# Two unused tiles that put the operands of every large matmul at multiples of 512 bytes

## The chip, the cores and the metric

The kernel runs on one core of one Trainium2 chip. The metric is device time in microseconds (us) of one execution; before the change the median of three runs is 2399.38 us (2398.85 to 2400.38).

## The reference

One decoder layer on 2048 tokens of width 1024, in float32. What matters here is that it is a chain of large matrix products, all of which TensorE computes:

```
h = rms_norm(x, norm_w) * (1 + scale) + shift          # shift, scale, gate = silu(c) @ w_ada + b_ada
z = h @ w_in                                            # 1024 -> 10240 columns
a, b, g_conv, q, k, v, g_attn, m_conv, m_attn = split(z)
u = silu(layer_norm(causal_conv31(a * sigmoid(b)))) * silu(g_conv)
y_conv = u @ w_conv_out
o = merge(dilated_attention(rope(norm(q)), rope(norm(k)), v))   # 12 heads, 3 dilations
y_attn = (o * silu(g_attn)) @ w_attn_out
y = sigmoid(m_conv) * y_conv + sigmoid(m_attn) * y_attn
out = x + gate * (y @ w_out)
```

## The kernel before

Every large product is made in three terms: each operand is split into a high part of type fp32r and the fp32r remainder (tiles with hi/lo or h/l in their names), and high*high, high*low and low*high are summed in one PSUM bank. One matmul loads a stationary operand of 128x128 and streams a moving operand past it, 384 or 512 columns wide. The order of TensorE's instructions is written out by hand (`tc.manual_schedule`), so PE goes through the program as it stands; the other engines are ordered by the tile scheduler. The stages, in order of time:

1. **Start** (L120 to L225): the condition vector, the angles of the rotary table, the first tokens' norms. Tiles in the pools `start` and `xp`.
2. **Token projection with attention** (L371, 4608 matmuls of 384 columns): 12 heads by 16 blocks of 128 tokens, 24 matmuls each into `pz`. Stationary is a 128-token slice of `hT_hi`/`hT_lo` (pools `hT0`, `hT1`), moving the weights `wh_u`/`wl_u` (pools `wp0`, `wp1`). Between the matmuls of a block stand those of attention: `ptq` (L436), `ps` (L451), `ptp` (L468) and `po` (L500), plain float32 of 128 columns, on tiles of the pool `wk` and the constant `ident`.
3. **Quads** (L897, 3696 matmuls of 512 columns): the convolution's and the gates' columns, two column blocks by two token blocks in seven products instead of eight (tiles A, S for tokens, B, T for weights), 12 matmuls a product. Moving are the token quarters in `hT0`/`hT1`, stationary the weights `sh`/`sl` in the pool `ws`.
4. **Projections back** (L1203, 1152 matmuls of 512 columns): 32 blocks `ya` of 12 matmuls, then 32 blocks `yc` of 24. Moving are the attention's or the convolution's output (`ai`, `u` in the pools `ub` and `ua`; for the first 8 `ya` blocks `ai0` in `hT0`), stationary `wa` and `wc` (in `hT0` and `wcp`). Beside them VectorE and ScalarE normalise the convolution's output for the next token quarter, which PE needs in two small steps, `pc` (L1239) and `pr` (L1248), and prepare the last stage's weights (`wo_raw`, L1349 and L1354).
5. **Output** (L1485, 672 matmuls of 512 columns): 8 quads of seven products of 12 matmuls into `oa`, `ob`, `oc`. Stationary is `y` (pool `ub`, the first two products `op`), moving the seven weight tiles `wo`: B11 in `lnp`, T2, B22 and T4 in `hT0`, T3 in `wcp`, B21 and T1 in `op`.

SBUF is given out as two stacks: pools opened without a side grow up from the low addresses ("left"), those with `side="right"` grow down from the top ("right"). A tile's start address is therefore the sum of what lies beneath it on its own side. The lines that set this around the change:

```
tab = tabs.tile([P, NB, 2, 64], F32, tag="tab", name="tab0")          # L120
with pool("start", side="right") as st:                               # L121
...
hpool_c = [tc.tile_pool(name=f"hT{i}", bufs=1, side="right", reuse_waits="tile") for i in range(2)]
...
gpa_c.__exit__(None, None, None)                                      # L1170
cv_c.__exit__(None, None, None)
gp = ctx.enter_context(pool("gt", bufs=3))
big["fr"] = ctx.enter_context(pool("fr", bufs=2))
...
wcp_c, wcp = right("wcp")
lnp_c, lnp = right("lnp")
ys_c = pool("ys", bufs=2)
up_c = [pool("ub"), pool("ua")]
...
            nc.tensor.matmul(pz, w, xx, start=(m == 0), stop=(m == len(terms) - 1))   # L1203
```

The three 512-column stages differ in nothing but tiles: L897, L1203 and L1485 all are a loop over 12 or 24 terms, with the next stationary operand loaded while the present moving one streams.

Of the kernel before, what the change touches and what calls it, by code (L numbers as in the profile page):

```python
# [10 lines left out]
F32 = mybir.dt.float32  # L11
# [7 lines left out]
P = 128  # L19
# [35 lines left out]
def tile_hybrid_block(  # L55
# [9 lines left out]
    def pool(name, bufs=1, **kw):  # L65
        return tc.tile_pool(name=name, bufs=bufs, reuse_waits="tile", **kw)
# [51 lines left out]
    tabs = tabs_c.__enter__()  # L118

    tab = tabs.tile([P, NB, 2, 64], F32, tag="tab", name="tab0")  # L120
    with pool("start", side="right") as st:  # L121
        keep = tc.keep_in_program_order
        nat = st.tile([4 * KC, P], F32, name="nat")
# [467 lines left out]
    side = {}  # L591
# [577 lines left out]
    assert not conv_todo  # L1169
    gpa_c.__exit__(None, None, None)  # L1170
    cv_c.__exit__(None, None, None)
    gp = ctx.enter_context(pool("gt", bufs=3))
    big["fr"] = ctx.enter_context(pool("fr", bufs=2))
    pe_order.__exit__(None, None, None)
# [399 lines left out]
```

## Time and profile before

| | |
|---|---|
| median of three runs | 2399.38 us |
| the profiled execution's own time | 2401.62 us |
| its span, first to last instruction | 2399.8 us |
| mean granted TensorE clock | 0.993 |
| PE / weight loads / VectorE / ScalarE / GpSimd busy | 98% / 87% / 72% / 43% / 35% |

Busy times of PE cannot be added to a time, since matmuls are pipelined and overlap: one of 512 columns is shown for some 0.39 us while the next starts 0.23 us after it. What a matmul costs is read from start to start, or from the chain of waits: there each piece is a run of the same kind, with its length and its count, and length divided by count is the price of one.

### The profile page before, as it was taken

What the parts mean: (1) busy time and instruction counts of PE and PEld (TensorE: products, weight loads), DVE (VectorE), ACT (ScalarE), POOL (GpSimd) and SP (SyncE); (2) the same over time, 40 slices, a digit from 0 to 9 for tenths busy, and PEclk for the clock granted to TensorE, in tenths of its full rate; (3) what the DMA queues carried; (4) which work ended last, traced back from release to release, by engine and by line L of the source; (5) the groups of instructions that cost most, each with busy time, mean ns of one, the idle gap of its engine ahead of it and who ended that gap; (6) DMA issues with size and microseconds to landing.
All of it is one profiled execution on the core that took longest, in us unless ns stands there. A gap on an engine that the chain in (4) does not pass through costs nothing.

```text
span 2399.8 us, 38725 instructions
## 1 busy us (share of the span) xinstructions
PE 2356.1 (98%) x12353; PEld 2089.2 (87%) x12353; DVE 1738.8 (72%) x4091; ACT 1022.4 (43%) x2850; POOL 842.7 (35%) x1003
## 2 busy tenths in 40 slices
PE   6999999999999999999999999999999999999999
PEld 2989999999999999998888888788888888878887
DVE  5865655655556777777699999979968778787544
ACT  4733433333444454456444444644444444332221
POOL 3421111111111111123667779656556730000221
PEclk8999999999999999999999999999999999999999
DMA  7633544555552222134545455745444579866552
GB/s 258 216 118 105 163 124 143 155 151 155 165 161 79 65 79 62 55 108 156 169 133 176 154 158 193 239 127 152 141 149 132 167 228 319 288 230 200 177 158 101
DMA packets 354105, 378.56 MB, mean 158 GB/s; under 512 B 29736, under 2 KB 251208, under 8 KB 353902
## 3 DMA queue, kind: packets, MB, share of 16 engines
q1 hardware_dynamic: 316414, 316.64, 42.4%
q10 hardware_dynamic: 37488, 59.46, 7.3%
q8 instruction: 98, 1.61, 0.3%
q14 instruction: 105, 0.86, 0.1%
HBM read 235.34 MB, written 140.64 MB: 157 GB/s over the span
## 4 chain that ended last, share of the span: by engine, by line
PE 87%; DVE 3%; DMA 2%; ACT 2%; issue 1%; POOL 1%; SPq 0%; ACTq 0%; DVEq 0%; POOLq 0%
PE pz L371 29%; PE paab L897 7%; PE yc L1203 6%; PE oa L1485 4%; PE ya L1203 4%; PE pcab L897 4%; PE pag_mc_d L897 4%; PE pag_g_d L897 3%; PE pag_ma_d L897 3%; PE po L500 3%; PE ps L451 3%; PE oc L1485 2%; PE pcg_g_d L897 2%; PE pcg_mc_d L897 2%; PE paag L897 2%; PE pbab L897 2%
## 5 line engine op out<-in xcount | busy, mean ns | idle before, releaser
L371 PE MATMUL pz<-wh_u,hT_lo 128*128 128x384 f32 x1536 | 536.8, 350 | 5.4 <-DVE hT_lo L290 3.6
L371 PE MATMUL pz<-wh_u,hT_hi 128*128 128x384 f32 x1536 | 518.7, 338 | 4.8 <-ACT wh_u L347 2.4
L371 PE MATMUL pz<-wl_u,hT_hi 128*128 128x384 f32 x1536 | 519.2, 338 | 0.4 <-DVE wl_u L350 0.4
L114 POOL TENSOR_SCALAR st<-st 128x2 f32<-128x2 f32 x192 | 48.6, 253 | 809.8 <-ACT sq L388 809.8
L402 DVE SCALAR_TENSOR_TENSOR qk<-pz,st,wqk 128x128 f32<-128x128 f32 x384 | 116.9, 346 | 270.7 <-POOL st L115 269.6
L371 PEld LDWEIGHTS pz<-wh_u,hT_hi 128*128 128x128 f32 x1536 | 291.0, 189 | 8.0 <-ACT wh_u L347 3.3
L371 PEld LDWEIGHTS pz<-wh_u,hT_lo 128*128 128x128 f32 x1536 | 290.0, 189 | 8.3 <-DVE hT_lo L290 4.6
L371 PEld LDWEIGHTS pz<-wl_u,hT_hi 128*128 128x128 f32 x1536 | 290.0, 189 | 1.6 <-DVE wl_u L350 1.1
L443 ACT ACTIVATE qkT<-ptq 128x256 f32<-128x256 f32 x192 | 73.5, 383 | 358.3 <-PE ptq L436 304.0
L975 DVE SCALAR_TENSOR_TENSOR ce<-us,pair_taps,ce 128x512 f32<-128x512 f32 x240 | 180.6, 753 | 6.5
L946 DVE SCALAR_TENSOR_TENSOR ce<-ut,chan,ce 128x512 f32<-128x512 f32 x240 | 178.7, 745 | 0.0
L861 POOL TENSOR_TENSOR slT<-wT,shT 128x512 fp32r<-128x512 f32 x107 | 143.7, 1344 | 81.0 <-ACT shT L860 81.0
L959 DVE SCALAR_TENSOR_TENSOR cq<-ut,chan,cq 128x512 f32<-128x512 f32 x208 | 155.2, 746 | 1.0
L860 ACT ACTIVATE shB<-wB 128x512 fp32r<-128x512 f32 x130 | 82.0, 631 | 162.7 <-PE paab L897 51.7
L115 POOL TENSOR_TENSOR st<-st,mhalf 128x2 f32<-128x2 f32 x192 | 137.3, 715 | 16.0
L388 ACT ACTIVATE sq<-pz 128x128 bf16<-128x128 f32 x384 | 105.6, 275 | 87.5 <-PE pz L371 78.5
L860 ACT ACTIVATE shT<-wT 128x512 fp32r<-128x512 f32 x110 | 69.4, 631 | 163.9 <-POOL wT L852 33.3
L861 POOL TENSOR_TENSOR slB<-wB,shB 128x512 fp32r<-128x512 f32 x85 | 111.0, 1306 | 77.9 <-ACT shB L860 77.4
L500 PE MATMUL po<-lv,pT 128*128 128x128 f32 x596 | 96.8, 274 | 0.0
L500 PEld LDWEIGHTS po<-lv,pT 128*128 128x128 f32 x596 | 90.9, 190 | 0.6 <-issue 0.5
L409 DVE TENSOR_TENSOR t<-qk,tab 128x256 f32<-128x256 f32 x192 | 82.4, 429 | 5.5
L861 POOL TENSOR_TENSOR slT<-wB,shT 128x512 fp32r<-128x512 f32 x57 | 75.1, 1322 | 27.5 <-ACT shT L860 27.4
(742 smaller groups left out, 6162.2 us busy)
## 6 DMA issues: line engine op xcount, KB each, us to landing
wB<-in_w_in_dram SPq DMA_DIRECT2D x154, 256.0 KB, 3.4
qkv_d<-qkv SPq DMA_DIRECT2D x128, 192.0 KB, 2.3
wT<-tT_d SPq DMA_DIRECT2D x88, 256.0 KB, 2.7
raw_u<-in_w_in_dram SPq DMA_DIRECT2D x93, 192.0 KB, 3.4
tT_d<-wB ACTq DMA_DIRECT2D x66, 256.0 KB, 2.3
lqk<-qkv_d SPq DMA_DIRECT2D x128, 128.0 KB, 2.2
acc_d<-osb SPq DMA_DIRECT2D x128, 65.0 KB, 2.0
part<-acc_d ACTq DMA_DIRECT2D x64, 130.0 KB, 2.2
```

Of the source, the lines that this page charges most:

```text
L115: nc.gpsimd.tensor_tensor(dst, scratch[:, :n], mhalf[:, :n], op=ALU.pow)
L371: nc.tensor.matmul(pz[:, :width], part(a, k, P * j, P), w[:, :width], start=(m == 0), stop=(m == 23))
L402: nc.vector.scalar_tensor_tensor(qk[:, 2 * i : 2 * i + 2].rearrange("p a b -> p (a b)"), pz[:, P * i : P * i + P], st[:, 2 + i : 3 + i], w ...
L500: nc.tensor.matmul(po[:, :P], box["pT"][:, P * i : P * i + P], vt, start=(i == 0), stop=(i == nk - 1))
L860: nc.scalar.activation(h, q[name], AF.Copy)
L861: eng.tensor_tensor(l, q[name], h.bitcast(F32), op=ALU.subtract)
L897: nc.tensor.matmul(ps, w, x, start=(m == 0 and ps.name not in first), stop=(m == 11 and not more), skip_group_check=True)
L946: stt(box["e"], e[:, 1 + j : 513 + j], chan[:, cb, 2 * j : 2 * j + 1], box["e"], op0=ALU.mult, op1=ALU.add)
L959: stt(box["o"], o[:, 2 + j : 514 + j], w, psum_o, op0=ALU.mult, op1=ALU.add)
L975: stt(dst, box["both"][:, 1 + j : 513 + j], pair_taps[:, cb, j : j + 1], box["e"], op0=ALU.mult, op1=ALU.subtract if j == 0 else ALU.add)
L1203: nc.tensor.matmul(pz, w, xx, start=(m == 0), stop=(m == len(terms) - 1))
L1485: nc.tensor.matmul(ps, y, w, start=(m == 0 and ps.name not in begun), stop=(m == 11 and not more), skip_group_check=True)
```

## The change

```
@@ -118,6 +118,8 @@
     tabs = tabs_c.__enter__()
 
     tab = tabs.tile([P, NB, 2, 64], F32, tag="tab", name="tab0")
+    edge = ctx.enter_context(pool("edge", side="right"))
+    edge.tile([P, 120], F32, name="edge")
     with pool("start", side="right") as st:
         keep = tc.keep_in_program_order
         nat = st.tile([4 * KC, P], F32, name="nat")
@@ -1169,6 +1171,8 @@
     assert not conv_todo
     gpa_c.__exit__(None, None, None)
     cv_c.__exit__(None, None, None)
+    level = ctx.enter_context(pool("level"))
+    level.tile([P, 32], F32, name="level")
     gp = ctx.enter_context(pool("gt", bufs=3))
     big["fr"] = ctx.enter_context(pool("fr", bufs=2))
     pe_order.__exit__(None, None, None)
```

`edge` takes 480 bytes of each partition at the top and so moves every right-hand tile of the whole program down by 480. `level` takes 128 bytes and moves the left-hand tiles that are opened after the quads (`gt`, `fr`, `ys`, `ub`, `ua`, `ap`, `op`) up by 128. Neither is read or written. On each of the five engines the same instructions on the same tiles stand in the same order before and after; only addresses differ, and a handful of semaphore waits that follow from which older tile a new one overlaps. The start of each operand within 512 bytes, from the two built programs:

| stage | matmuls | moving, before -> after | stationary, before -> after |
|---|---|---|---|
| token projection L371 | 4608 | `wh_u`, `wl_u` 480 -> 0 | `hT` 480 -> 0 |
| quads L897 | 3696 | quarters 480 -> 0 | `sh`, `sl` 480 -> 0 |
| L1203, first 8 `ya` blocks | 96 | `ai0` 480 -> 0 | `wa` 480 -> 0 |
| L1203, the rest | 1056 | `ai`, `u` 384 -> 0 | `wa`, `wc` 480 -> 0 |
| L1485, B11, T2, T3, B22, T4 | 480 | `wo` 480 -> 0 | `y` 384 -> 0 |
| L1485, B21 and T1 | 192 | `wo` 384 -> 0 | `y` 384 -> 0 |
| attention L436 to L500 | | `ident` 128, `wk` tiles 256 and 416, unchanged | the same |

Of the waits, three matter: one fetch `part<-acc_d` (L516, ScalarE's queue, second block of the ninth head) now also waits for the store `s_d` of the last quarter sum; the first `d<-pm,d` (L1229, VectorE) also waits for a GpSimd instruction of the last quad (L923); and the load `yq` (L1395, SyncE's queue) and one `ai` remainder no longer wait for GpSimd.

More of the change, by code (lines that the diff above doesn't have):

```diff
@@ L120, in tile_hybrid_block @@
     tab = tabs.tile([P, NB, 2, 64], F32, tag="tab", name="tab0")
+    edge = ctx.enter_context(pool("edge", side="right"))
+    edge.tile([P, 120], F32, name="edge")
     with pool("start", side="right") as st:
@@ L1171, in tile_hybrid_block @@
     cv_c.__exit__(None, None, None)
+    level = ctx.enter_context(pool("level"))
+    level.tile([P, 32], F32, name="level")
     gp = ctx.enter_context(pool("gt", bufs=3))
```

## The prediction

> **What bounds the kernel.** I read the page first: the busy shares, the clock, and the chain that ended last.
>
> ```profile
> span 2399.8 us, 38725 instructions
> PE 2356.1 (98%) x12353; PEld 2089.2 (87%) x12353; DVE 1738.8 (72%) x4091; ACT 1022.4 (43%) x2850; POOL 842.7 (35%) x1003
> PEclk8999999999999999999999999999999999999999
> ...
> PE 87%; DVE 3%; DMA 2%; ACT 2%; issue 1%; POOL 1%; SPq 0%; ACTq 0%; DVEq 0%; POOLq 0%
> ```
>
> TensorE is the bound: 87% of the chain is PE, at full clock almost everywhere. Nothing in this change adds or removes a matmul, so the only question is whether the price of one matmul depends on where its operands start. For that I read the chain of waits stretch by stretch (columns: start in us, length in us, engine, tile, line, count) and divide length by count. First the quads, where by the table of the change both operands start at 480:
>
> ```profile
> 1302.33 2.72 PE pag_mc_d L897 x12
> ...
> 1326.81 2.72 PE paab L897 x12
> ```
>
> 2.72 us over 12 is 226.7 ns for 512 columns. Now the stage behind it, whose first pieces are of the same shape:
>
> ```profile
> 1960.32 7.26 PE ya L1203 x32
> ...
> 2004.43 33.73 PE ya L1203 x144
> ...
> 2056.27 33.73 PE yc L1203 x144
> ...
> 2146.89 92.78 PE yc L1203 x396
> ```
>
> The first 32 matmuls have `ai0` at 480 against `wa` at 480: 7.26/32 = 226.9 ns, as in the quads. The later ones have the moving operand at 384 against a stationary one at 480: 33.73/144 = 234.2 ns, twice, and 92.78/396 = 234.3 ns. Same stage, same width, same weights `wa`; what differs is where the moving tile lies. Last, the output stage:
>
> ```profile
> 2245.21 2.81 PE oa L1485 x12
> 2248.02 2.76 PE ob L1485 x12
> 2250.78 2.81 PE oa L1485 x12
> ...
> 2262.00 2.76 PE oc L1485 x12
> 2264.76 2.81 PE oa L1485 x12
> ...
> 2396.06 0.69 DVE xt L1472
> ```
>
> Here the stationary `y` is at 384. Products with weights at 480 (all `oa`) take 2.81/12 = 234.2 ns; those with weights at 384 (`ob`, and the `oc` at 2262.00) 2.76/12 = 230.0 ns. Inside such an `ob` the timeline (start, shown length, matmul) tells why it lies between:
>
> ```profile
> 2247.86 0.40 PE L1485 MATMUL ob<-wohB,yh 128*128 128x512 f32 x1
> ...
> 2249.72 0.39 PE L1485 MATMUL ob<-wohB,yl 128*128 128x512 f32 x1
> ...
> 2250.62 0.40 PE L1485 MATMUL oa<-wohT,yh 128*128 128x512 f32 x1
> ```
>
> The first eight steps take 1.86 us, 232.5 ns each; the last four 0.90 us, 225 ns each to the rounding. Equal starts do not give the low price at once: the stream falls into it after some eight matmuls. So I read a rhythm between the two streams, cheap when moving and stationary operand start at the same place within 512 bytes, and reached only after several matmuls. Distance is not the cause: by their addresses the operands of the quads lie 20 to 184 KB apart, those of the dear pairs 59 to 190.
>
> **The change part by part.** `level` and `edge` together bring the 384s and 480s to one value, 0.
>
> *L1203.* 1152 matmuls less the 96 already equal are 1056, at 234.2 - 226.9 = 7.3 ns: **-7.7 us**.
>
> *L1485.* A quad of 84 matmuls recurs every 2264.76 - 2245.21 = 19.55 us. At 2.72 us for 12, it takes 7 x 2.72 = 19.04. That is 0.51 us for each of 8 quads: **-4.1 us**.
>
> Does the whole gain show? Waits of PE in this part, and the stretches where other engines might become late:
>
> ```profile
> PEld pr L1248 <- POOL stf L115: 2.0, 1, 2.0
> ```
>
> ```profile
> 1981.00:2052.00 71.00, 71.00 (x320) 57.50 (x319) 52.60 (x86) 27.31 (x45) 2.90 (x4) 1.00 0.96 326
> 2104.00:2134.00 30.00, 30.00 (x128) 23.80 (x127) 26.70 (x43) 12.57 (x20) 0.00 (x0) 1.00 0.58 193
> 2236.00:2396.00 160.00, 160.00 (x688) 128.89 (x686) 82.59 (x119) 34.06 (x61) 39.52 (x29) 1.00 0.46 147
> ```
>
> ```profile
> 2135.53 9.13 DMA wo_raw<-in_w_out_dram
> 2144.65 1.03 POOL stf L115
> 2145.69 0.04 issue
> 2145.73 1.16 PE pr L1248 x8
> ```
>
> (Windows: stretch, length, busy us of PE, PEld, DVE, ACT, POOL, clock, DMA share, GB/s.) In the output stage PE never waits and the others are half idle: its 4.1 us come out whole, since behind the last matmul stands one VectorE addition. In L1203 PE waits once, 2.0 us before `pr`: VectorE is nearly full there (26.70 of 30 us), held up by the load `wo_raw`, and its small `stf` chain stands behind that. Whatever of this chain doesn't follow PE leaves the wait longer. The chain before it was begun by the previous `pr`, eight `yc` blocks or 192 matmuls earlier (`pr` is due at blocks 7 and 15), so PE gains at most 192 x 7.3 ns = 1.4 us on it. Between 0 and 1.4 I take **+1.0**: the last steps of this chain are DMA, DVE and SyncE's queue, not PE. The DMA engines are nearly full from 1981 to 2052 (0.96), but PE waited for nothing there, and gains only 2 us over it; I take 0.
>
> *Projection and quads.* Both operands move by the same 480, so their relation stays. The price at equal 384 (225 ns, rounded), at equal 480 in the quads (226.7) and in L1203 (226.9) is one price within the rounding, so the common start seems not to matter: I take 0. The rows differ by 0.2 ns, over 8304 matmuls 1.7 us either way. One thing does change here: attention tiles stay at 128, 256 and 416, and the rhythm is found anew after each attention piece.
>
> ```profile
> 602.74 0.33 PE L371 MATMUL pz<-wh_u,hT_hi 128*128 128x384 f32 x1
> ...
> 604.15 0.33 PE L371 MATMUL pz<-wh_u,hT_lo 128*128 128x384 f32 x1
> ...
> 605.89 0.33 PE L371 MATMUL pz<-wh_u,hT_hi 128*128 128x384 f32 x1
> ```
>
> Eight steps in 1.41 us (176 ns), then ten in 1.74 (174 ns): some 18 ns lost in a piece, in 192 blocks 3.5 us. At best this goes, at worst it doubles; I take 0.
>
> *Start.* DMA targets and ScalarE's and VectorE's operands move too. In the start PE waits 10.6 us for `wada`:
>
> ```profile
>   DMA wada<-in_w_ada_dram: 10.6, 2
> ```
>
> No row shows a load that depends on its target's start. All of that wait gone is one end, as much again the other; I take 0, nearest to the rest of the trace, where nothing points either way.
>
> *Waits.* The fetch at L516 now waits for a store; the next fetch behind it in ScalarE's queue waited already for a later DMA on the same semaphore, so ScalarE, and PE behind its `qkT`, can't lose more than that wait. L1229, behind which on VectorE stand the sums that lead to `pc`, waits for a GpSimd instruction of the quads' end, and needs `pm`, which PE computes at the fourth `ya` block; GpSimd has no instruction by then, as the row below shows. The waits dropped are not on the path. 0 for all of them.
>
> ```profile
> 1960.00:1980.00 20.00, 20.00 (x88) 16.20 (x87) 13.86 (x23) 7.19 (x13) 0.00 (x0) 1.00 0.98 316
> ```
>
> Sum: -7.7 - 4.1 + 1.0 = **-10.8 us**. Against the profiled execution's own 2401.62 us (span 2399.8) that is 2390.8; this execution lies 2.2 us above the median of the runs, so against 2399.38 it is **2388.6 us**, 0.45% less.
>
> *A rule against it.* The Trainium skill, "TensorE: Matmul & The Clock Gate", Part 2 (What happens when you issue a matmul), says that PE has two independent read ports and that loading the next weights takes no bandwidth from the running matmul. By that rule operand positions could not matter, and the sum would be 0. The trace disagrees: 226.9 and 234.2 ns stand in one stage. The same page's gap between warm back-to-back matmuls, 215.7 ns at 512 columns, is met by neither.
>
> **Rivals.**
>
> *No effect (2399 us).* The price follows something else that goes with the tiles, such as the side of SBUF, and both starting at 0 changes nothing. For it: all cheap pairs but one lie wholly on the right side. Against it: that one, both operands on the left at 384, reaches 225 ns. That the tiles would not move as said is excluded by the addresses.
>
> *Gain eaten (2393 to 2397 us).* PE runs into VectorE and the DMA queues, which L1203 fills: PE's wait before `pr` grows by more than 1.4 us, or new waits appear at `yc`. At most all 7.7 of L1203 is lost: 2399.4 - 4.1 = 2395.3.
>
> *Multiples of 512 are special (2340 to 2380 us).* From 384 to 512 columns the settled price rises from 174 to 226.7 ns, 0.41 ns a column; 512 columns at that rate are 211 ns, so some 16 ns of each matmul don't depend on its width. If a start at 0 saved part of that, all 10128 matmuls would gain: each nanosecond is 10.1 us, and the 8304 that I hold at 0 give 8.3 us of it. With the steps seen here, 230.0 to 226.7, it would be 27 us: 2361. Against it: 384 and 480, of which one is a multiple of 128 and the other only of 32, cost the same.
>
> *Slower.* One place: the token projection. `hT` and `wh_u` at 0 stand in another relation to the attention tiles, and if from there the rhythm is not found within a block's run of matmuls, as it never is in `oa`, the 4608 pay up to 7.3 ns, 33.6 us: 2422. It outweighs the gain from 10.8 us / 4608 = 2.3 ns each. Against it: today it is found from 128, 256 and 416 alike within eight matmuls.
>
> **How the numbers follow.** Forecast 70%, 2383 to 2394. Gain eaten 9%. Multiples special 9%. No effect 6%. Slower 6%. The range takes in the forecast with the re-locking term and half the start's (2388.6 - 3.5 - 1.7 - 5.3, down to 2378; the start's full ends, which no row supports, stay out), the eaten gain and the upper edge of the special case: **2377 to 2397 us**, which holds the forecast, the eaten gain and a sliver of the special case, some 81%. About 0.2%, 4.8 us, is what a measurement of this kernel can tell from no change, so faster means under 2394.6: most of the forecast (0.69), half of the eaten gain (0.05), all of the special case (0.09): 0.83. The same: the rest of both, no effect, and a little of the slower case: 0.12. Slower: 0.05.
>
> **What would show it.** In the chain after: the pieces of 144 at L1203 32.7 us instead of 33.73; every product of 12 in the output stage 2.72 us, `oa` and `ob` alike, the quad 19.0; the quads' 2.72 and the projection's steps unchanged; the wait before `pr` at 2 to 3.4 us, and no second one. It would be wrong if L1203 or `oa` stayed at 234 ns, if the quads moved off 226.7, or if PE waited more than it saved.

## The result, and the profile after

The changed kernel takes 2392.55 us (median of six runs, 2388.53 to 2393.74) against 2399.69 for the kernel before beside it: a ratio of 0.9967, 95% interval 0.9957 to 0.9978. That is 7.1 us less, where 10.8 were predicted. The profiled execution is the fastest of the six, 2388.53 us (span 2386.7).

The page of the changed kernel, busy shares and chain:

```profile
span 2386.7 us, 38725 instructions
PE 2343.6 (98%) x12353; PEld 2088.3 (87%) x12353; DVE 1737.6 (73%) x4091; ACT 1024.4 (43%) x2850; POOL 843.8 (35%) x1003
...
PE 89%; DVE 3%; DMA 3%; ACT 2%; POOL 1%; issue 1%; SPq 0%; ACTq 0%; DVEq 0%; POOLq 0%
```

TensorE is still the bound, and its busy time fell by 12.5 us (2356.1 to 2343.6). The chain of waits of the changed kernel (start, length, engine, tile, line, count) shows where; L1207 and L1489 are the old L1203 and L1485:

```profile
1952.14 2.72 PE pcg_ma_d L899 x12
...
1957.58 7.26 PE ya L1207 x32
...
2001.10 32.67 PE ya L1207 x144
...
2052.30 32.67 PE yc L1207 x144
...
2140.75 89.82 PE yc L1207 x396
2230.57 2.72 PE oa L1489 x12
2233.30 2.72 PE oc L1489 x12
```

The pieces of 144 fell from 33.73 to 32.67 us, 226.9 ns a matmul; the 396 from 92.78 to 89.82, 226.8 ns. Every product of the output stage now takes 2.72 us, `oa` (2.81 before) like the others. The quads' 2.72 and the first 32 `ya` at 7.26 did not move. Both forecast terms are there in full size.

Two things are there that the forecast did not have. The first is PE's waits between 1950 and 2160 us (tile, line, releaser; us, times, longest), of the kernel before and then of the changed one:

```profile
PE pr L1248 <- POOL stf L115: 1.6, 1, 1.6
```

```profile
PE pr L1252 <- POOL stf L115: 1.6, 2, 1.0
PE pc L1243 <- DVE red L1237: 0.7, 1, 0.7
```

The wait before `pr` is no longer than before (the 2.0 us of the prediction are the row of the weight load ahead of `pr`; PE itself stood for 1.6), but PE also waits before `pc`, for VectorE's sum `red`. The second is in the token projection. Pieces of the chain, of the kernel before and then of the changed one, near its begin and its end:

```profile
248.40 4.17 PE pz L371 x24
...
1030.52 4.17 PE pz L371 x24
```

```profile
250.98 4.19 PE pz L373 x24
...
1030.11 4.19 PE pz L373 x24
```

A run of 24 matmuls behind an attention piece costs 0.02 us more. From the start of the 864th of the 4608 matmuls to the start of the 4320th, the changed kernel loses 2.54 us on the kernel before.

Last, the profiled execution lies 4 us below its median partly for a reason outside the change: the granted clock, 0.996 in the mean against 0.993 to 0.995 in the other five. The stretches 120 to 160 and 1100 to 1165 us (stretch, length, busy of PE, PEld, DVE, ACT, POOL, clock, DMA share, GB/s), before and after:

```profile
120.00:160.00 40.00, 35.16 (x189) 31.94 (x188) 26.17 (x71) 14.94 (x55) 11.11 (x16) 0.96 0.41 131
1100.00:1165.00 65.00, 61.10 (x288) 50.39 (x287) 34.57 (x84) 40.60 (x83) 26.02 (x25) 0.97 0.59 188
```

```profile
120.00:160.00 40.00, 35.27 (x195) 32.51 (x196) 26.00 (x73) 14.17 (x55) 10.95 (x16) 1.00 0.40 129
1100.00:1165.00 65.00, 59.86 (x290) 49.53 (x289) 34.09 (x82) 39.87 (x80) 26.93 (x25) 1.00 0.58 188
```

In these two stretches the granted clock is lower in the kernel before and full in the changed one; which of them are hit differs from one execution of the same kernel to the next (0.97 from 1100 to 1165 in the second profile of the changed kernel also). Single profiles are therefore compared by stage below, and totals by medians.

### The profile page after: what moved, and what is told of

The parts are those of the page before. It is cut to its first block, busy times and chain, and to the rows that moved or that the text cites. A ratio compares the mean times of both kernels' runs of the same rounds, so it can differ in the third digit from the quotient of the medians.

```text
span 2386.7 us, 38725 instructions
## 1 busy us (share of the span) xinstructions
PE 2343.6 (98%) x12353; PEld 2088.3 (87%) x12353; DVE 1737.6 (73%) x4091; ACT 1024.4 (43%) x2850; POOL 843.8 (35%) x1003
## 4 chain that ended last, share of the span: by engine, by line
PE 89%; DVE 3%; DMA 3%; ACT 2%; POOL 1%; issue 1%; SPq 0%; ACTq 0%; DVEq 0%; POOLq 0%
PE pz L373 31%; PE paab L899 7%; PE yc L1207 5%; PE pcab L899 4%; PE pag_mc_d L899 4%; PE oa L1489 4%; PE pag_g_d L899 3%; PE ya L1207 3%; PE pag_ma_d L899 3%; PE po L502 3%; PE ps L453 3%; PE pcg_g_d L899 2%; PE oc L1489 2%; PE pbab L899 2%; PE paag L899 2%; PE pcg_mc_d L899 2%
```

## The experiments

Two theories stood at first. **A**: what counts is the distance of the moving operand's start from the stationary one's, and the projection's loss comes from its distance to the attention tiles. **B**: a start at a multiple of 512 counts by itself. After the first four runs came **G**: the faster PE runs into VectorE, which loads hold up. Each version is measured beside the kernel before on the same chip, whose medians are: 2400.80 us beside `right_only`, `level_only`, `equal_480` and `all_shift`, 2400.53 beside `after_again`, `scale_late`, `all_480_scale_late` and `distances`, 2400.12 beside the other four. Each name stands at its run below.

### One pad alone

The changed kernel without `level` (`right_only`):

```
-    level = ctx.enter_context(pool("level"))
-    level.tile([P, 32], F32, name="level")
```

> Only the right-hand pad of 120 floats is kept: stationary operands of the merge products and moving ones of the output stage start at 0 modulo 512, their partners at 384, so the distance is 128 instead of 96 and 0. Theory A (what counts is the distance of the two starts modulo 512): the merge products stay near 234 ns in the mean and the quads near 19.55 us, and the token projection loses the 2.5 us that it lost in the changed kernel: 2402 us. If the distance counts modulo 128 instead, 128 is as good as 0: merge products at 227 ns, and the time is that of the changed kernel, 2392.6 us. Theory B (a right-hand start at a multiple of 512 is good by itself): part of the gain, merge products below 231 ns, 2394 to 2398 us.

Measured 2400.34 us, ratio 0.9998 (0.9989 to 1.0007). Its chain:

```profile
2004.47 33.59 PE ya L1205 x144
...
2238.38 2.80 PE oa L1487 x12
2241.18 2.73 PE oc L1487 x12
```

33.59/144 is 233.3 ns: with the distance 128 the price is that of a mismatch, and B is out. The projection lost 2.56 us between the 864th and the 4320th matmul, as in the changed kernel, though nothing but `edge` was changed. So that loss belongs to `edge`. Next, the changed kernel without `edge` (`level_only`):

```
-    edge = ctx.enter_context(pool("edge", side="right"))
-    edge.tile([P, 120], F32, name="edge")
```

> Only the left-hand pad of 32 floats is kept: the left-hand operands start at 0, the right-hand ones at 480, a distance of 32. Theory A: merge products in the mismatch mixture, 231 to 238 ns, output quads 19.5 us, token projection as before: 2399.7 us within 3. Theory B (one operand at a multiple of 512 is enough, or half of the gain): merge products at 227 to 231 ns, 2389 to 2395 us.

Measured 2399.75 us, 0.9995 (0.9986 to 1.0004):

```profile
2057.86 33.60 PE yc L1205 x144
...
2146.89 92.39 PE yc L1205 x396
```

92.39/396 is 233.3 ns at the distance 32, and the projection is as before (0.07 us). As A had it.

### Equal starts, but not at a multiple of 512

The changed kernel without `edge`, and with a smaller `level` (`equal_480`):

```
-    edge = ctx.enter_context(pool("edge", side="right"))
-    edge.tile([P, 120], F32, name="edge")
...
-    level.tile([P, 32], F32, name="level")
+    level.tile([P, 24], F32, name="level")
```

> No right-hand pad, and a left-hand one of 24 floats in place of 32: both operands of the merge products and of the output products start at 480 modulo 512, none at a multiple of 512. Theory A (equal starts are what counts): merge products 227 ns, output products 2.72 us per 12, and the token projection as before the change, since nothing of it moves: 2399.7 - 10.4 = 2389.3 us, some 3 us better than the changed kernel. Theory B (the multiple of 512 counts): merge products at 234 ns and 2399.7 us.

Measured 2394.43 us (2390.80 to 2398.53), 0.9974 (0.9962 to 0.9985). By its prices this is as A said. The chain of this version between 2105 and 2232 us:

```profile
2117.96 4.21 DMA gg<-g_d
2122.21 1.22 DVE wo_raw L1356
...
2136.79 0.61 DVE red L1235
2137.53 1.84 PE pc L1241 x8
2139.37 7.59 PE yc L1205 x24
2146.97 0.89 PE pr L1250 x8
2147.86 84.37 PE yc L1205 x372
```

84.37/372 is 226.8 ns, with both operands at 480. The projection is back at the old time (0.05 us). But the total misses A's 2389.3 by 5 us, and the same rows say why: the chain comes to `pc` by way of a load, a gate multiply on VectorE and `red`. VectorE's timeline shows that this multiply itself stood for its own load, and PE's what came of it:

```profile
2121.07 2.36 DVE L1356 TENSOR_TENSOR wo_raw<-wo_raw,gate 128x1024 f32<-128x1024 f32 x2 [1.94 <-DMA wo_raw<-in_w_out_dram]
...
2137.53 1.84 PE L1241 MATMUL pc<-ones,red 128*128 128x1 f32 x8 [3.07 <-DVE red L1235]
...
2140.66 0.63 PE L1205 MATMUL yc<-u_5h,wc1h 128*128 128x512 f32 x1
2141.09 0.63 PE L1205 MATMUL yc<-u_5l,wc1h 128*128 128x512 f32 x1
```

PE stood for 3.07 us, and the matmuls behind the wait start 0.43 us apart, where they cost 0.23: the wait was followed by a stretch at half clock (the mean granted clock is 0.89 from 2130 to 2160, and 1.00 in the kernel before). Between the 726th and the 792nd matmul of that line this version loses 3.84 us on the kernel before, whose own wait before `pr` lies in the same place. This gave theory G. The kernel before shows how little room there was:

```profile
2135.39 0.68 DVE L1233 TENSOR_TENSOR red<-red,sq 128x512 f32<-128x512 f32 x1
...
2137.46 0.94 PE L1239 MATMUL pc<-ones,red 128*128 128x1 f32 x8
```

The last addition to `red` ended at 2136.07 us, and PE came to `pc` 1.4 us later. Of the merge matmuls, 636 that become cheaper stand before this `pc`; at 7.3 ns each PE can come 4.6 us earlier. If `red` came no earlier at all, PE would wait 3.2 us.

### All older left-hand tiles moved along

The changed kernel with a pad beneath all left-hand tiles (`all_shift`):

```
+    consts.tile([P, 8], F32, name="pad")
     ident = consts.tile([P, P], F32, name="ident")
...
-    level.tile([P, 32], F32, name="level")
+    level.tile([P, 24], F32, name="level")
```

> As the changed kernel (both operands of the late stages at 0, the token projection at 0 and 0), but every left-hand tile that is older than the pad is moved by 32 bytes too, so that the tiles of the attention pieces keep the distance to the token projection's tiles that they had before the change. Theory A with its second half (the token projection lost 2.5 us because its distance to the attention operands changed): the stretch of the token projection is back at the old time, and the whole is 2389.3 us. Rival (its start at 0 itself is what costs after an attention piece, or the loss is noise of one profile): the stretch stays 2.5 us longer, 2392.6 us.

Measured 2391.75 us (2389.81 to 2397.39), 0.9966 (0.9953 to 0.9978). Pieces of its projection:

```profile
248.21 4.17 PE pz L374 x24
...
1030.34 4.17 PE pz L374 x24
```

4.17 again, and 0.02 us of loss between the two marks: with both starts at 0 the projection costs what it did, if the attention tiles keep their distance. Its total is 2.5 us above A's, with a wait of 3.4 us at `pc` in its profile.

### The changed kernel once more

This is `after_again`:

> The changed kernel as it is, beside the kernel before on the chip that runs the next three. Theory A expects 2392 to 2393 us and, in its token projection, the same 2.5 us of loss between the 864th and the 4320th matmul against the kernel before; if that loss were an accident of one profile, it would be within 0.3 us of zero here. Theory G (the faster PE runs into VectorE, which is held by the loads of the output weights) expects PE to wait at the column sums pc of the norm again, 0.5 to 3.5 us.

Measured 2395.72 us (eleven runs, 2390.31 to 2400.17), 0.9975 (0.9966 to 0.9984). PE's waits and the window of the second profile:

```profile
PE pr L1252 <- POOL stf L115: 2.4, 2, 1.8
PE pc L1243 <- DVE red L1237: 2.3, 1, 2.3
```

```profile
2130.00:2160.00 30.00, 25.85 (x114) 20.95 (x114) 25.43 (x40) 8.78 (x14) 1.62 (x2) 0.94 0.79 264
```

The projection's loss is 2.55 us again, no accident. The waits add up to 4.7 us here, with a lower clock behind them, and the whole gain is 4.8 us instead of 7.1. How much of its gain the change keeps varies with these waits.

### The gate multiplies behind `red`

The scheduler had put VectorE's gate multiply of the first output weight, which waits for its load, between the additions to `red` of the last token quarter. Here that is changed, on the version with all late starts at 480 (`scale_late`):

```
-                    nc.vector.tensor_add(self.red, self.red, sq)
+                    add = nc.vector.tensor_add(self.red, self.red, sq)
+                    if t == 3:
+                        tc.keep_in_program_order(add)
...
-            nc.vector.tensor_tensor(w[:, :, c], w[:, :, c], last["gate"][c][:, None, :].to_broadcast([P, 2, 512]), op=ALU.mult)
+            tc.keep_in_program_order(nc.vector.tensor_tensor(w[:, :, c], w[:, :, c], last["gate"][c][:, None, :].to_broadcast([P, 2, 512]), op=ALU.mult))
```

> The version with all starts at 480, and on VectorE the gate multiplies of the output weights (line 1356 there) are kept behind the last addition to red for the fourth token group; nothing is left out. Theory G (what PE waits for at pc is VectorE, held up by a gate multiply that waits for its DMA): the wait of 3.1 us at pc and the half clock behind it go, and the kernel gains 3 to 4 us in the profile against that version: 2389 to 2391 us. Rival: the wait at pc is the loads gg of the norm alone; then it stays at 2 us or more and the time at 2394 us. A second risk is that the output weights are prepared too late, which would show as a wait of PE before oa.

Measured 2390.03 us (2388.70 to 2390.42), 0.9953 (0.9940 to 0.9965). Its window and its chain:

```profile
2130.00:2160.00 30.00, 30.00 (x142) 25.08 (x141) 19.71 (x31) 8.62 (x13) 1.26 (x2) 1.00 0.75 257
```

```profile
2134.22 0.79 PE pc L1243 x8
2135.00 5.61 PE yc L1205 x24
2140.61 0.89 PE pr L1252 x8
2141.50 86.41 PE yc L1205 x381
```

PE is busy for all 30 us at full clock, and neither `pc` nor `pr` is waited for there. As G had it; the rival, the loads `gg` alone, is out, since VectorE still waited 3.1 us for `gg` in this run. PE waits once for 0.5 us before `oa`, for an output weight, but it did so in `equal_480` too, so the reordering did not cause it. The median fell by 4.4 us against the same starts without the reordering, though not beside the same runs.

To see whether the reordering is a gain of its own, the same edit was made on the kernel before (`before_scale_late`):

> The kernel before, with only the order on VectorE changed (the gate multiplies behind the last addition to red); all starts as before the change. Theory G (the late gate multiplies only matter once PE is fast enough to run into them): the kernel before did not wait at pc, so this gives at most the 1.6 us of its wait at pr, 2398 to 2400.5 us. Rival (the reordering is a gain of its own, whatever the starts): it gains the 5 us that it gained on the aligned kernel, 2395 us.

Measured 2398.81 us, 0.9994 (0.9985 to 1.0003): not told apart from no change. And on the changed kernel (`after_scale_late`):

> The changed kernel with that same order on VectorE. Theory G: its wait at pc and the half clock behind it go, so that it shows the whole gain of the merge and output products less the 2.5 us of the token projection: 2391 to 2392.5 us, some 2 us above the same with all starts at 480 (2390.0 us). If the wait at pc was not what cost the changed kernel 5 us against that, it stays at 2395 us.

Measured 2388.53 us (2385.88 to 2389.82), 0.9950 (0.9937 to 0.9962). PE's only wait from 1950 us to the end, and pieces of the chain:

```profile
PE pr L1254 <- POOL stf L115: 0.2, 1, 0.2
```

```profile
2103.64 27.23 PE yc L1207 x120
...
2138.16 89.80 PE yc L1207 x396
2227.95 2.72 PE oa L1491 x12
```

So the reordering is worth 1.3 us on the kernel before, not told apart from nothing, and 4 to 7 us on the changed one (2388.53 against 2392.55 and 2395.72, which were measured beside other runs). By its median this is the fastest version measured, 11.6 us under the kernel before. G's forecast of 2391 to 2392.5 for it was some 3 us too high: by the trace the reordering also takes away 1.4 of the 1.6 us of wait before `pr` that the kernel before had; the rest of the difference is not explained.

### Attention operands at 480 too, or 64 bytes further

On `scale_late`, the attention tiles were padded to start at 480 (`all_480_scale_late`; `ident` and the pool `wk` moved, 352 bytes put behind `osb`):

```
+    consts.tile([P, 88], F32, name="pad")
...
+    wk.tile([P, 96], F32, tag="padw", name="padw", bufs=1)
...
+                wk_pad.append(wk.tile([P, 88], F32, tag="pado", name="pado", bufs=1))
...
-    level.tile([P, 24], F32, name="level")
+    level.tile([P, 64], F32, name="level")
```

> As the run before this one, and the operands of the attention pieces (identity, q and k, scores, values) are padded so that they too start at 480 modulo 512. Theory A with its second half (what a token projection matmul pays after an attention piece depends on the distance of the new starts from the old ones): the excess over 173.3 ns of the first ten matmuls behind a piece, now 12.6 ns after the first interval, falls to under 5 ns, worth 1.5 to 2.4 us over some 190 pieces; 2387 to 2389 us. Rival (re-locking comes from the other shape, 128 columns, and not from the starts): the excess stays at 12 ns or grows, and the time is that of the run before this one.

In another version (`attention_64`) they lie 64 bytes further from the projection's tiles than in the kernel before:

```
+    consts.tile([P, 16], F32, name="pad")
...
-    level.tile([P, 24], F32, name="level")
+    level.tile([P, 8], F32, name="level")
```

> As the version with all late starts at 480 and the late gate multiplies, but with the attention pieces' tiles 64 bytes further from the token projection's. Theory A's second half, as far as it stands (the cost of re-locking is some function of the distance to the attention operands): the ten matmuls behind a piece cost something other than 99.0 ns (the old distance) and 112.5 ns (32 bytes less), and the token projection changes by about 190 pieces times the difference. If the cost went with something else, it stays at 99 ns.

Measured 2389.45 us (0.9952, 0.9938 to 0.9965) and, in a single run, 2393.01 us. What tells is the excess over 173.3 ns of the `pz` intervals behind an attention piece, mean of 166 or 167 pieces that end in `ptq`, worked out from the starts in the traces, in ns (the sums move by up to 2 ns with the choice of pieces that are left out):

```
interval                   1st   2nd  3rd  4th  5th  6th  7th  8th   2nd to 10th   864th to 4320th, us
kernel before             86.4  -0.4  0.8  2.2  4.5  1.9  3.0  0.5       12.6           0
all_shift                 86.4  -0.4  0.8  2.1  4.4  1.8  3.1  0.4       12.5         +0.02
changed kernel            86.7  -0.6  2.6  6.7  7.7  4.4  4.9  0.0       25.8         +2.54
attention at 480          85.1   2.1  5.1  2.4  4.3  3.1  0.7  1.8       19.5         +0.81
attention 64 further      85.0   2.2  4.6  2.1  4.4  3.0  1.0  1.7       19.3         +1.05
```

Every version with the old distance between attention and projection tiles pays 12.4 to 12.8, those with `edge` and unmoved attention tiles 25.7 to 25.8: 13 ns for each of the 188 pieces that end in `ptq` are 2.4 us, about the loss. That re-locking depends on this distance is shown. That equal starts make it cheap is wrong: at 480 and 480 it costs more than the old 128, 256 and 416. Which distance is cheapest, and why, stays open. The second version also shows that the reordering does not remove every wait at `pc`: PE waited there once, 1.0 us, for the `red` of an earlier token quarter.

### More distances

Pads of 64 and 80 floats beneath `ub` and `ua` in `equal_480` (`distances`), then of 48 and 104 (`distances_2`):

```
     up = [c.__enter__() for c in up_c][::-1]
+    up[1].tile([P, 64], F32, name="pad_b")
+    up[0].tile([P, 80], F32, name="pad_a")
```

> The version with all starts at 480, with the left-hand operands moved away: 256 bytes apart from the right-hand ones in the odd token groups of the merge and in the output stage, 64 bytes apart in the even groups. 32, 96 and 128 bytes gave 233.4, 234.3 and 232.9 ns per merge product. If the relation repeats every 256 bytes, the 256 groups are at 227 ns; if it repeats every 64, the 64 groups are; if only every 512, both are at 232 to 235 ns. In that case some 2401 us.

> More distances between the starts: 192 bytes in the odd token groups, 96 in the even ones, and 320 in the output stage. Theory A corrected (the relation repeats every 256 bytes, as 256 cost no more than 0): 320 costs what 64 did, about 229 ns per product in the output stage, 192 is the mirror of 64 and costs about 229 ns, and 96 costs 233 to 235 ns. Without a mirror, 192 lies at 231 to 235 ns.

Measured 2395.10 and 2398.38 us in a single run each. From the first, the even token quarters (64 apart) and a product of the output stage (256 apart); then from the second a piece of L1207 (192 apart, but for its first 6 matmuls at 96) and two products of the output stage (320 apart, 64 modulo 256):

```profile
2055.81 32.97 PE yc L1207 x144
...
2236.40 2.72 PE oa L1489 x12
```

```profile
2003.70 33.61 PE ya L1207 x144
...
2238.32 2.76 PE oa L1489 x12
2241.08 2.75 PE oc L1489 x12
```

256 apart costs as little as 0, so the relation repeats every 256 bytes, not 512, which was the first of the three cases; the 2401 us belonged to the third. 32.97/144 is 229.0 ns at 64; 2.76/12 and 2.75/12 are 229 to 230 at 320; 33.61/144 is 233.4. Mean intervals of all runs, by moving start minus stationary start modulo 256:

```
bytes        0      32     64     96     128    160    192    224
ns         227.0  233.4  229.1  233.4  232.9  234.3  233.3  233.4
```

Only 0 is cheap, 64 lies a third of the way up, and its mirror 192 is dear. Why the two streams should agree modulo 256 bytes, no run shows.

## Why the prediction was nearly right, step by step

**L1203, -7.7, and the output stage, -4.1: right.** The traces give 1056 x (234.26 - 227.02) ns = 7.6 us, and 4.0 us over the 672 output matmuls. That equal starts count, and not multiples of 512, is shown by the version at 480; the period of 512 was wrong, it is 256.

**Token projection 0: the mis-sized term.** It costs +2.54 us, inside the bound of 3.5. The prediction saw the mechanism, re-locking behind attention pieces, and found no reason for either sign. The loss goes when the attention tiles move along.

**Give-back +1.0, and "no second one": tied to the wrong place, and in the second profile too small.** The step took PE's wait before `pr` as the only one and bounded the loss by what a chain that starts with the previous `pr` can fall behind. But `pc` has a chain of its own, VectorE's `red`, which goes through `gg` and `wo_raw` loads that need not come earlier when PE does, and it had 1.4 us of room against 4.6 us of gain. In the first profile the merge stage gives back 7.6 - 6.3 = 1.3 us, of which 0.7 are the wait at `pc`; in the second it gains only 2.3, so 5.3 are given back, of which 2.3 are the wait at `pc`, 1.8 the lower clock behind it (0.94 over 30 us) and 0.8 longer waits before `pr` (2.4 in all, from 1.6); 0.4 are left over. This is the rival "gain eaten", taken at 9%: its mechanism is real and takes part of the gain in both profiles. That the first measurement, 2392.55, fell into the forecast and just short of this rival's 2393 to 2397 was in part luck: measured again on another chip, the same kernel took 2395.72, inside the rival's range.

**The start, 0: nothing found against it.** The first `pz` comes 1.8 to 2.1 us earlier than in the kernel before's profile in four of the five profiles with `edge`, and 1.8 to 2.3 earlier in six of the eight without it, the reordered kernel before among them. So the difference is the spread of that stage, not the moved starts.

The sum with the measured terms is -7.6 - 4.0 + 2.5 + 1.3 = -7.8 for the first profile, against a median of -7.1; with 5.3 it is -3.8, against -4.8. Of the other rivals, no effect and multiples of 512 are refuted; the slower one had the right place and a thirteenth of its price.

What stays open: the version with all starts at 480 does without the projection's 2.5 us, and yet its median with the reordering, 2390.03, is not below 2388.53 of the changed kernel with it. They were not run side by side, with five runs each, and one profile of the first shows 1.2 us of wait before `pr` against 0.2. The two profiles cannot settle it. They lie 4.1 us apart, and TensorE's granted clock was halved for 23.9 us of the projection and the quads in the first and for 11.3 in the second, which alone is worth up to 6.3 us. Beside that the output stage took 152.9 us against 152.1, with the wait of 0.5 us before `oa` in the first alone.

## What to carry to other kernels

Price one matmul by start-to-start time for each pair of pools; two prices for the same shape point to where the operands start. Before counting a gain in a stage where VectorE and the loads are nearly full, look for every wait point of PE in it, not only for the one that waits now, and ask which of its feeders wait for loads instead of PE. Pinning one multiply that the scheduler had put ahead of a short sum that PE needs was worth about as much as the alignment's missing part.

## What the runs showed of the hardware

An fp32r matmul of 512 columns costs 226.7 to 227.0 ns when moving and stationary operand start at the same place modulo 256 bytes, 229 at 64 bytes, and 233 to 234 at the other six multiples of 32. Behind the plain float32 matmuls of attention, the settled price of a 384-column matmul (173.3 ns) is regained over some seven matmuls, at 12.5 to 25.8 ns in all beside a first interval that is 85 to 87 ns longer; the sum depends on the starts. And a wait of PE of 3.1 us was followed by matmuls at 0.43 us instead of 0.23, so that it cost more than its length: 3.84 us against a place where the kernel before itself waits 1.6.
